# A two-layer diffusion trunk on one core: the order on each engine set by the kernel's own list scheduler

## The chip, the cores and the metric

The kernel runs on one core of a Trainium2 chip. A core has a matrix engine (TensorE, here PE), a vector engine (VectorE, DVE), a scalar engine with function tables (ScalarE, ACT), a general engine (GpSimd, POOL) and a queue that issues most transfers (SyncE, SP). Each engine works through its own list of instructions in the order of the list and waits on semaphores for the others. The metric is the device time of one launch in microseconds; times are medians of several runs. The profile is of one execution of its own.

## The reference: what is computed

Two layers over 512 latent tokens and 256 context tokens of width 1024. Each layer is a mixing part and an MLP, both with RMS norms and modulation vectors made from a conditioning vector. The mixing part projects to four branches (windowed attention A, neighbourhood attention B, and two bidirectional gated recurrences C and D), multiplies each with its branch weights and a gate, adds them, and multiplies with w_out. In the last layer the context is only read.

```
h  = rms_norm(x, ng[0]) * (1 + sc1) + sh1          # hc likewise, for the context
z  = split_in(h @ w_in)                            # queries, keys, values, decays, gates
y  = merge([window(A), neighbourhood(B), recurrence(C), recurrence(D)], z['merge'])
     # merge: sum over j of sigmoid(gate_j) * (branch_j @ w_branch[j]), then @ w_out
x  = x + g1 * rms_norm(y, ng[1])
h2 = rms_norm(x, ng[2]) * (1 + sc2) + sh2
x  = x + g2 * rms_norm(relu(h2 @ w1)**2 @ w2, ng[3])
```

The recurrence of C (4 heads, key width 128) and D (4 heads, key width 64) is a sum over earlier tokens weighted with products of per-channel decays, in both directions.

## The kernel before, in words

Everything is computed by one `Builder`, whose methods issue instructions to `nc.tensor`, `nc.vector`, `nc.scalar`, `nc.gpsimd` and `nc.sync`.

*Weights.* The large weights come as 342 pieces of 128 x 1024 (`wr`), loaded by SP. Each is split into a high part `wh` (ACT, L78, a copy to a rounded format) and a low part `wl` (DVE, L79, the difference). A product is then three passes of matmuls (`mm3`, L433; tiles `pd`): low input by high weight (`hTl,wh`), high by low (`hTh,wl`), high by high (`hTh,wh`). The tiles `hTh` and `hTl` are the normalised tokens, transposed. The MLP's second product goes over `gff` (L1396, tile `y`).

*Norms.* Tokens are normalised in rows (`xn`, DVE L397), transposed on PE (`xT`, L401), scaled by the modulation and split into `hTh` and `hTl` (L414).

*Recurrences.* `d_decays` makes the decays of the d heads on ACT and DVE (tiles `Fe`, `F`, L698 to L705). ACT uses functions of several tables there (exponential, logarithm), and a change of table is an instruction of its own, ACT_TABLE_LOAD. `scan` works on one c head or on two d heads (rows 0 to 63 and 64 to 127 of one tile). It treats tokens in levels of growing distance. At a level, ACT copies the keys `KC` (L563), PE makes for each head one product per block of 128 tokens into the tile `lev` (L579; the two first levels L573 with `pr` and `ones`), DVE rescales `QP` and `KR` by the decays (L583, L584), and DVE copies each head's products by mask into `AT` (L596). There are six blocks in layer 0 and four in layer 1. A matmul on data of four-byte precision with a 128-column output is two PE instructions in the profile.

*Attention B* works on pairs of heads: scores `bS` (PE, L1058 and L1059), the bias table added (DVE, L1063), the maximum `bnm` (DVE, L1065), exponentials `bP` with their sums (ACT, L1068), 1/sum `brl` and scaling (DVE, L1071, L1073), transposes `pT` (PE, L831), the split of the transposed weights into `PTh` (ACT, L834) and `PTl` (DVE, L835), and the output `bO` (PE, L1098).

*Branches.* `pd` from `ysp` and the branch weights is multiplied with its gate into `gates` (DVE, L1165) and added to `acc` (L1166). At the same time DVE makes the modulation vectors of the next part: dot products `mj` of `wm` rows with the conditioning row `cb` (`mod_dot`, L226).

*Order.* Work of one kind is written as Python generators (`self.side`), and the main loop advances them by hand between matmuls (`step`), so that PE has projections to do while a scan or an attention goes on. Tiles come from pools with a fixed number of buffers (PSUM: three `pd`, two `S` tiles of two banks, one `q`). The framework under the kernel takes the program so written, adds the semaphores, and places the instructions of each engine.

## Time and profile before

| | us |
|---|---|
| median of the timed runs (3 runs, 3159.12 to 3166.61) | 3165.26 |
| the profiled execution's own time | 3156.36 |
| its span in the profile | 3154.6 |
| PE busy / DVE busy / ACT busy | 3028.0 / 2074.1 / 1230.0 |
| mean granted clock of PE | 0.994 of full speed |

Busy time is the time in which an engine has at least one instruction in work. "Idle before" in a row is how long the engine stood still ahead of the instruction, and what released it. PEld is PE's loading of weights, which runs beside its products.

### The profile page before, as it was taken

To read this page: it belongs to the slowest core of one execution; us is meant where nothing else is said; L and a number is where in the kernel's file an instruction comes from. 1 tells how busy PE (TensorE), PEld (TensorE's weight loads), DVE (VectorE), ACT (ScalarE), POOL (GpSimd) and SP (SyncE) were. 2 spreads that over 40 slices of the span, in tenths; PEclk is the share of its full clock that TensorE was granted. 3 is DMA by queue.
4 is the path that set the end of the run, shared out by engine and by line. 5 is a ranking of instruction groups with operands and counts; after the bars stand their busy time and mean duration, and the time that the engine had idled before them with its cause. 6 is when DMAs were issued, how large, how long until landed. Compare 5 with 4: busy or idle time off the path is not lost.

```text
span 3154.6 us, 42754 instructions
## 1 busy us (share of the span) xinstructions
PE 3028.0 (96%) x17236; PEld 2746.2 (87%) x17236; DVE 2074.1 (66%) x3313; ACT 1230.0 (39%) x2214; POOL 78.2 (2%) x120
## 2 busy tenths in 40 slices
PE   4999999999989999999999989999999999989998
PEld 3999999999989997898989878898888888778887
DVE  7756675377687666587664555677478577656555
ACT  4523332255525542522222354233256355342222
POOL 1000000000000000000000000000000000000000
PEclk9999999999999999999999999999999999999999
DMA  6111111201252223344331221111221223444332
GB/s 219 61 34 36 46 48 54 71 28 40 81 174 64 74 84 117 118 141 160 121 108 66 88 96 53 42 47 61 83 75 61 91 65 95 155 143 138 98 100 94
DMA packets 77782, 278.21 MB, mean 88 GB/s; under 512 B 9496, under 2 KB 9640, under 8 KB 77584
## 3 DMA queue, kind: packets, MB, share of 16 engines
q1 hardware_dynamic: 74112, 267.47, 25.5%
q0 software_dynamic: 3328, 8.00, 1.3%
q8 instruction: 136, 2.23, 0.3%
q14 instruction: 62, 0.51, 0.1%
q10 hardware_dynamic: 144, 0.01, 0.0%
HBM read 257.08 MB, written 10.49 MB: 85 GB/s over the span
## 4 chain that ended last, share of the span: by engine, by line
PE 46%; DVE 8%; ACT 2%; DMA 2%; issue 2%; POOL 0%; POOLq 0%; DVEq 0%; ACTq 0%; SPq 0%
PE pd L433 27%; PE y L1396 11%; DVE wl L79 1%; PE lev L579 1%; PE o L635 1%; PE pd L1293 1%; DMA wm<-in_wmT 1%; DVE xt L1325 1%; PE pd L1396 1%; DVE mj L226 1%; PE U L616 1%; POOL rstd L387 0%; PE pT L925 0%; PE aO L956 0%; DVE macc L285 0%
## 5 line engine op out<-in xcount | busy, mean ns | idle before, releaser
L433 PE MATMUL pd<-hTh,wl 128*128 128x384 f32 (+2 forms) x2992 | 653.7, 351 | 0.5 <-DVE wl L79 0.5
L433 PE MATMUL pd<-hTl,wh 128*128 128x384 f32 (+3 forms) x2992 | 632.1, 351 | 14.7 <-DVE hTl L414 10.4
L433 PE MATMUL pd<-hTh,wh 128*128 128x384 f32 (+2 forms) x2992 | 615.0, 346 | 0.0
L79 DVE TENSOR_TENSOR wl<-wr,wh 128x1024 fp32r<-128x1024 f32 x342 | 415.0, 1221 | 246.2 <-ACT wh L78 239.0
L433 PEld LDWEIGHTS pd<-hTl,wh 128*128 128x128 f32 (+1 forms) x2992 | 521.7, 189 | 46.5 <-DVE hTl L414 12.5
L433 PEld LDWEIGHTS pd<-hTh,wh 128*128 128x128 f32 x2992 | 529.4, 189 | 26.2 <-issue 0.4
L433 PEld LDWEIGHTS pd<-hTh,wl 128*128 128x128 f32 x2992 | 523.9, 190 | 29.2 <-issue 3.1
L78 ACT ACTIVATE wh<-wr 128x1024 fp32r<-128x1024 f32 x342 | 358.0, 1055 | 413.0 <-PE y L1396 312.7
L1396 PE MATMUL y<-wh,gff 128*128 128x512 f32 x1120 | 300.0, 390 | 0.0
L1396 PEld LDWEIGHTS y<-wh,gff 128*128 128x128 f32 x1120 | 210.2, 188 | 44.5
L1402 DVE TENSOR_TENSOR y<-y,y 128x1024 f32<-128x1024 f32 x130 | 158.1, 1220 | 124.9 <-PE y L1396 124.9
L433 PE MATMUL pd<-ysp,wh 128*128 128x384 f32 (+1 forms) x768 | 179.6, 362 | 17.4 <-DVE gates L1165 14.7
L1396 PE MATMUL y<-wl,gff 128*128 128x512 f32 x560 | 174.2, 391 | 1.9 <-DVE y L1402 1.2
L433 PEld LDWEIGHTS pd<-ysp,wh 128*128 128x128 f32 x768 | 137.5, 190 | 31.5 <-DVE gates L1165 15.9
L1353 ACT ACTIVATE relu<-pd 128x384 f32<-128x384 f32 (+2 forms) x100 | 51.3, 513 | 261.8 <-PE pd L433 261.8
L226 DVE SCALAR_TENSOR_TENSOR mj<-wm,cb 128x1024 f32<-128x1024 f32 x112 | 137.0, 1223 | 9.9 <-DMA wm<-in_wmT 9.0
L1396 PEld LDWEIGHTS y<-wl,gff 128*128 128x128 f32 x560 | 104.5, 188 | 24.9 <-DVE y L1402 3.2
L579 PEld LDWEIGHTS lev<-QP,KC 64*128 64x128 f32 (+1 forms) x960 | 107.6, 189 | 12.5 <-issue 6.7
L579 PE MATMUL lev<-QP,KC 64*128 64x128 f32 (+1 forms) x960 | 115.3, 281 | 3.2 <-DVE QP L584 2.4
L1355 DVE TENSOR_TENSOR relu<-relu 128x384 f32<-128x384 f32 (+2 forms) x100 | 58.1, 582 | 78.7 <-ACT gff L1354 78.7
L596 DVE COPY_PREDICATED AT<-lmask,lev 128x768 f32<-128x768 uint8 (+1 forms) x112 | 97.5, 877 | 10.2 <-PE lev L579 8.3
L387 POOL TENSOR_TENSOR rstd<-rstd,mhalf 128x1 f32<-128x1 f32 (+2 forms) x58 | 47.8, 825 | 1791.3 <-DVE rstd L386 1788.6
(283 smaller groups left out, 4032.0 us busy)
## 6 DMA issues: line engine op xcount, KB each, us to landing
wr<-in_wp SPq DMA_DIRECT2D x342, 512.0 KB, 3.5
wm<-in_wmT SPq DMA_DIRECT2D x64, 512.0 KB, 4.0
wm<-in_wmg SPq DMA_DIRECT2D x32, 512.0 KB, 3.6
xd<-xt SPq DMA_DIRECT2D x16, 512.0 KB, 3.0
xt<-xd SPq DMA_DIRECT2D x14, 512.0 KB, 4.0
btab<-in_btab SPq DMA_DIRECT2D x8, 768.0 KB, 6.9
xt<-in_x SPq DMA_DIRECT2D x8, 512.0 KB, 4.4
bkh<-bkh POOLq DMA_DIRECT2D x16, 192.0 KB, 4.1
```

The lines of the kernel that those rows point to most:

```text
L78: nc.scalar.activation(hi, raw, AF.Copy)
L79: nc.vector.tensor_tensor(lo, raw, hi.bitcast(F32), op=ALU.subtract)
L226: nc.vector.scalar_tensor_tensor(junk, t, 1.0, c, op0=ALU.mult, op1=ALU.mult, accum_out=dst[:, w:w + 1])
L387: nc.gpsimd.tensor_tensor(r[:, :n], r[:, :n], self.mhalf[:, :n], op=ALU.pow)
L433: nc.tensor.matmul(ps[:M, :n], w(k)[:, :M], h(k, t0, n), start=(i == 0), stop=(i == tot - 1))
L579: nc.tensor.matmul(ps[:, c], KC[r0:r0 + dk, c], self.comb_ap(QP[r0:r0 + dk], b, blk, 1), start=True, stop=True)
L596: nc.vector.copy_predicated(at[:, :n].rearrange("p (k t) -> p k t", k=nout), self.lmask[:, lev, None, :].to_broadcast([128, nout, 128]), p ...
L616: nc.tensor.matmul(us[r0:r0 + dk, j * 128:(j + 1) * 128], KT[:, j * 128 + r0:j * 128 + r0 + dk], zs[:, sq[j] * 128:(sq[j] + 1) * 128], sta ...
L1353: nc.scalar.activation(r[:, :m], ps[:, :m], AF.Relu)
L1355: nc.vector.tensor_tensor(r[:, :m], r[:, :m], r[:, :m], op=ALU.mult)
L1396: nc.tensor.matmul(ps, gts[lo + e][:, a_ * NTOK + t * 128:a_ * NTOK + (t + 1) * 128], ws[e][w_][:, h * 512:(h + 1) * 512], start=(i == 0), ...
L1402: nc.vector.tensor_tensor(d, d, ps2, op=ALU.add)
```

## The change

Builder's `nc` becomes a `Recorder`. Every call on one of its five engines is stored as a node instead of being issued. For each node it works out which earlier nodes must come first from the regions of the tiles that are read and written; a PSUM tile counts as one region, and two nodes on different engines that touch the same PSUM tile are ordered even when both read it. It also gives each node an occupancy and a latency from formulas with fixed numbers. When the program is complete, `order()` plays the five engines against these numbers: at each step it takes the engine that can start first, and on it the ready node that stands first in the program. There are two exceptions. On PE, after a matmul that uses at most 64 rows or columns of the array, ready nodes of the same shape go first, those of the half that is free earliest ahead. On ACT, nodes that need no other function table go first, for up to 3 us. `emit()` then issues the nodes in the order found and ties each one to the one ahead of it on its engine, without a semaphore. The formulas decide only the order; they do not change an instruction. In the changed kernel every instruction is issued at one line, L430.

```diff
+SEM = {("PE", "PE"): 0, ("ACT", "PE"): 52, ("DVE", "PE"): 55, ("POOL", "PE"): 54, ("DMA", "PE"): 60}
...
+class Engine:
+    def __getattr__(self, op):
+        rec, f, name = self.rec, getattr(self.real, op), self.name
+
+        def call(*a, **k):
+            rec.add(name, op, f, a, k)
+        return call
...
+    def depend(self, nd, r, w, preds):
+        name, p0, p1, m = r
+        bank = m < 0
...
+            if (w or ow or bank and o.eng != nd.eng) and o is not nd and q0 < p1 and p0 < q1 and (om & m):
...
+            if op == "matmul" and min(rows, m) <= 64 and rhs.dtype == F32:
+
+                nd.shape = "rows" if rows <= 64 else "columns"
+                t = lhs if rows <= 64 else o
+                nd.place = int(t.offset // list(t.ap)[0][0] >= 64)
...
+            nd.table = {"Exp": ("E",), "Tanh": ("E", "S"), "Sigmoid": ("S",), "Ln": ("L",)}.get(str(a[2]).split(".")[-1])
...
+    def order(self):
...
+                if R:
+                    c = (t, R[0][0], R[0][1], e, 0)
+                    if e == "PE" and shape:
+
+                        ok = [(free[N[x[1]].place],) + x for x in R if N[x[1]].shape == shape]
+                        if ok:
+                            c = (t,) + min(ok)[1:] + (e, 0)
+                    if e == "ACT" and N[c[2]].table and table not in N[c[2]].table and t - N[c[2]].ready < 3000:
+
+                        ok = [x for x in R if not N[x[1]].table or table in N[x[1]].table]
+                        if ok:
+                            c = (t,) + min(ok) + (e, 0)
+                elif L:
+                    c = (L[0][0], L[0][1], L[0][2], e, 1)
...
+    def emit(self, tc):
+
+        keep = mybir.DependencyInfo(mybir.DependencyClass.NoSync, mybir.DependencyReason.DATA)
+        last = {}
+        for nd in self.out:
+            f, a, k = nd.emit
+            ins = f(*a, **k).ins
+            if nd.eng in last:
+                tc.add_manual_dep(ins, last[nd.eng], keep, reason="order")
+            last[nd.eng] = ins.name
...
-        self.tc, self.nc, self.a = tc, tc.nc, a
+        self.tc, self.nc, self.a = tc, Recorder(tc.nc), a
...
+            self.nc.order()
+            self.nc.emit(tc)
```

Three places of the order, before and after. The rows give the place in the engine's list, the line, the operation, output<-inputs, the size, and the semaphores waited for.

**PE, the d heads' levels in layer 0**, before. `lev_1083` and `lev_1090` are the products of the two heads at one level; `pd` is a projection of other work.

```order
269 L433 MATMUL pd_1068<-hTh_159,wl_808 128x384 x4
270 L579 MATMUL lev_1083<-QP_950,KC_1081 128x128 [waits DVE_49,Activation_49]
271 L579 MATMUL lev_1083<-QP_950,KC_1081 128x128 x5
272 L579 MATMUL lev_1090<-QP_950,KC_1081 128x128 [waits DVE_49,PE_49]
273 L579 MATMUL lev_1090<-QP_950,KC_1081 128x128 x5
274 L433 MATMUL pd_1068<-hTh_159,wl_808 128x384 x4
275 L433 MATMUL pd_1068<-hTh_159,wh_807 128x384 x8
```

After; here `lev_274` and `lev_275` are the two heads of the same level.

```order
278 L430 MATMUL pd_272<-hTh_125,wl_239 128x384 x4
279 L430 MATMUL lev_274<-QP_256,KC_273 128x128 [waits DVE_49,Activation_49]
280 L430 MATMUL lev_274<-QP_256,KC_273 128x128 x3
281 L430 MATMUL lev_275<-QP_256,KC_273 128x128 [waits DVE_49,PE_49]
282 L430 MATMUL lev_274<-QP_256,KC_273 128x128
283 L430 MATMUL lev_275<-QP_256,KC_273 128x128
284 L430 MATMUL lev_274<-QP_256,KC_273 128x128
285 L430 MATMUL lev_275<-QP_256,KC_273 128x128 x4
286 L430 MATMUL pd_272<-hTh_125,wl_239 128x384 x4
287 L430 MATMUL pd_272<-hTh_125,wh_238 128x384 x8
```

Before, one head's six products stand ahead of the other's. After, the last two of the first head take turns with the first two of the second, and at the level that follows (`lev_277`, `lev_278`) the heads take turns from the first product to the last. The `pd` rows are where they were.

**DVE, attention B in layer 1**, before. `bS_21269` is the unit whose scores get their table here, `pT_21287` the transposes of the unit ahead of it.

```order
2607 L1063 TENSOR_TENSOR bS_21269<-bS_21269,btab_21188 128x2x256 [waits PE_49]
2608 L79 TENSOR_TENSOR wl_21301<-wr_21134,wh_21300 128x1024 [waits DMAHW6_49,Activation_49]
2609 L1065 TENSOR_REDUCE bnm_21222<-bS_21269 128x2 [waits DVE_49]
2610 L1071 RECIPROCAL brl_21283<-bl_21223 128x2 [waits Activation_49]
2611 L1073 TENSOR_SCALAR bP_21270<-bP_21270,brl_21283 128x512 [waits DVE_49]
2612 L1073 TENSOR_SCALAR bP_21270<-bP_21270,brl_21283 128x512
2613 L835 TENSOR_TENSOR PTl_21297<-pT_21287,PTh_21296 128x1024 [waits Activation_49]
2614 L1063 TENSOR_TENSOR bS_21319<-bS_21319,btab_21188 128x2x256 [waits PE_49]
2615 L782 TENSOR_TENSOR bkl_21167<-pd_21306,bkh_21166 64x6x64 [waits Activation_49]
2616 L1065 TENSOR_REDUCE bnm_21222<-bS_21319 128x2 [waits DVE_49]
```

After; the same unit is `bS_3098`, and the transposes ahead of it are `pT_3101`.

```order
2611 L430 TENSOR_TENSOR bS_3098<-bS_3098,btab_3087 128x2x256 [waits PE_49]
2612 L430 TENSOR_REDUCE bnm_3092<-bS_3098 128x2 [waits DVE_49]
2613 L430 TENSOR_TENSOR wl_3105<-wr_3077,wh_3104 128x1024 [waits DMAHW6_49,Activation_49]
2614 L430 TENSOR_TENSOR PTl_3103<-pT_3101,PTh_3102 128x1024 [waits Activation_49]
2615 L430 RECIPROCAL brl_3100<-bl_3093 128x2 [waits Activation_49]
2616 L430 TENSOR_SCALAR bP_3099<-bP_3099,brl_3100 128x512 [waits DVE_49]
2617 L430 TENSOR_SCALAR bP_3099<-bP_3099,brl_3100 128x512
2618 L430 TENSOR_TENSOR bS_3108<-bS_3108,btab_3087 128x2x256 [waits PE_49]
2619 L430 TENSOR_REDUCE bnm_3092<-bS_3108 128x2 [waits DVE_49]
2620 L430 TENSOR_TENSOR bkl_3081<-pd_3107,bkh_3080 64x6x64 [waits Activation_49]
2621 L430 TENSOR_TENSOR PTl_3113<-pT_3111,PTh_3112 128x1024 [waits Activation_49]
```

The maximum `bnm` has moved ahead of the weight split `wl`, and `PTl` of the unit ahead stands in front of `brl` and the scaling of `bP`, not behind them; one `bkl` has moved behind the next unit's scaling.

**DVE, the fourth branch in layer 0**, before. `gates` is the product of a branch's result with its gate, `mj` a dot product for the modulation.

```order
1000 L1166 TENSOR_TENSOR acc_3671<-acc_3671,gates_6825 128x384 [waits DVE_49]
1001 L226 SCALAR_TENSOR_TENSOR mj_7689,mods_96<-wm_7872,cb_7686 128x1024 [waits DVE_49]
1002 L79 TENSOR_TENSOR wl_7915<-wr_7753,wh_7914 128x1024 [waits DMAHW4_49,Activation_49]
1003 L226 SCALAR_TENSOR_TENSOR mj_7689,mods_96<-wm_7891,cb_7685 128x1024 [waits DMAHW4_49,DVE_49]
1004 L1165 SCALAR_TENSOR_TENSOR gates_6826<-gates_6826,pd_7920 128x384 [waits PE_49]
1005 L226 SCALAR_TENSOR_TENSOR mj_7689,mods_96<-wm_7891,cb_7686 128x1024 [waits DVE_49]
1006 L1166 TENSOR_TENSOR acc_3672<-acc_3672,gates_6826 128x384 [waits DVE_49]
```

After; `gates_1044` is the same gate.

```order
997 L430 TENSOR_TENSOR acc_603<-acc_603,gates_1043 128x384
998 L430 SCALAR_TENSOR_TENSOR mj_1182,mods_96<-wm_1207,cb_1180 128x1024 [waits DMAHW3_49,DVE_49]
999 L430 TENSOR_TENSOR wl_1213<-wr_1192,wh_1212 128x1024 [waits DMAHW4_49,Activation_49]
1000 L430 SCALAR_TENSOR_TENSOR mj_1182,mods_96<-wm_1207,cb_1181 128x1024 [waits DVE_49]
1001 L430 SCALAR_TENSOR_TENSOR gates_1044<-gates_1044,pd_1215 128x384 [waits PE_49]
1002 L430 SCALAR_TENSOR_TENSOR mj_1182,mods_96<-wm_1209,cb_1180 128x1024 [waits DMAHW4_49,DVE_49]
1003 L430 TENSOR_TENSOR acc_604<-acc_604,gates_1044 128x384 [waits DVE_49]
```

One `mj` that stood ahead of the `gates` product now stands behind it, and one `acc` addition ahead has moved up.

## Rows read from the trace of the kernel before

**Rows 1.** The page, part 1: busy time, share of the span and instructions per engine.

```profile
PE 3028.0 (96%) x17236; PEld 2746.2 (87%) x17236; DVE 2074.1 (66%) x3313; ACT 1230.0 (39%) x2214; POOL 78.2 (2%) x120
```

**Rows 2.** Windows: stretch, length, busy time per engine (instructions), granted clock, DMA share, GB/s.

```profile
86.00:3100.00 3014.00, 2938.91 (x16823) 2673.70 (x16823) 1976.13 (x3111) 1172.33 (x2104) 65.68 (x94) 0.99 0.26 85
870.00:935.00 65.00, 56.23 (x307) 53.89 (x307) 61.35 (x108) 10.75 (x14) 0.00 (x0) 0.97 0.54 171
935.00:1085.00 150.00, 139.90 (x975) 134.90 (x975) 111.57 (x180) 86.61 (x178) 8.24 (x16) 0.99 0.26 76
1790.00:1915.00 125.00, 110.61 (x569) 97.44 (x567) 74.85 (x128) 71.03 (x118) 7.81 (x12) 0.95 0.29 97
2495.00:2650.00 155.00, 146.70 (x962) 135.78 (x961) 107.48 (x150) 82.11 (x141) 8.16 (x16) 1.00 0.34 87
2735.00:2805.00 70.00, 61.70 (x318) 52.47 (x317) 42.14 (x76) 32.69 (x62) 5.37 (x9) 0.94 0.43 148
```

**Rows 3.** Waits of PE: waiting line, releaser: us in total, times, longest us.

```profile
PE pd L433 <- DVE gates L1165: 15.6, 11, 3.0
PE xT L401 <- DVE xn L397: 11.8, 11, 3.0
...
PE pT L831 <- DVE PTl L835: 7.4, 7, 1.3
PE bS L1058 <- ACT bP L1068: 4.8, 8, 1.2
```

**Rows 4.** Timeline of PE, d then c heads: start us, length us, line, tiles, count.

```profile
121.75 0.98 PE L573 MATMUL lev<-pr,ones 64*128 64x512 f32 x8
...
133.18 2.60 PE L579 MATMUL lev<-QP,KC 64*128 64x128 f32 x24
...
138.02 2.60 PE L579 MATMUL lev<-QP,KC 64*128 64x128 f32 x24
...
371.00 1.50 PE L579 MATMUL lev<-QP,KC 128*128 128x128 f32 x12
...
411.11 0.86 PE L573 MATMUL lev<-pr,ones 128*128 128x512 f32 x4
```

**Rows 5.** Instructions of tile lev: duration ns min/median/max, first and last start us, forms.

```profile
L579 PE MATMUL lev<-QP,KC x960: 270/275/387, 128.2 to 2225.4; 64*128 64x128 f32 x96, 128*128 128x128 f32 x96
```

**Rows 6.** Timeline of DVE between two such runs.

```profile
135.82 0.96 DVE L584 TENSOR_TENSOR QP<-QP,PT 128x768 f32<-128x768 f32 x1
...
136.70 1.02 DVE L596 COPY_PREDICATED AT<-lmask,lev 128x768 f32<-128x768 uint8 x1
```

**Rows 7.** Timeline of attention B, two units, layer 1 [idle before, releaser].

```profile
2542.70 0.69 ACT L1068 ACTIVATE bP<-bS,bnm 128x512 f32<-128x512 f32 x1 [2.49 <-DVE bnm L1065]
...
2543.04 1.20 PE L433 MATMUL pd<-hTh,wh 128*128 128x384 f32 x6
...
2545.19 1.22 DVE L835 TENSOR_TENSOR PTl<-pT,PTh 128x1024 fp32r<-128x1024 f32 x1
...
2550.43 0.39 PE L1058 MATMUL bS<-bkl,bq 128*128 128x256 f32 x1 [0.43 <-ACT bP L1068]
...
2551.53 1.23 DVE L835 TENSOR_TENSOR PTl<-pT,PTh 128x1024 fp32r<-128x1024 f32 x1
...
2552.81 1.09 PE L831 MATMUL pT<-ident,bP 128*128 128x128 f32 x8 [1.16 <-DVE PTl L835]
```

**Rows 8.** Timeline of the branch stage of layer 0.

```profile
912.32 1.23 DVE L226 SCALAR_TENSOR_TENSOR mj<-wm,cb 128x1024 f32<-128x1024 f32 x1
...
914.09 0.96 PE L433 MATMUL pd<-ysp,wh 128*128 128x384 f32 x4 [2.50 <-DVE gates L1165]
...
917.41 0.76 PE L433 MATMUL pd<-hTl,wh 128*128 128x384 f32 x3 [0.94 <-DVE gates L1165]
```

**Rows 9.** Timeline at the decays of the d heads, layer 1.

```profile
1907.48 1.28 ACT L492 ACT_TABLE_LOAD   x1
1907.52 1.00 PEld L433 LDWEIGHTS pd<-hTl,wh 128*128 128x128 f32 x8 [1.71 <-ACT wh L78]
```

320 lines of the change are left out of this document (added).

## The prediction

> **What bounds the kernel now.** I read the page first, then the windows by stage, then the table of waits, and last the timelines of the stages where TensorE (PE) stands idle. The page says that PE is busy 96% of the span, VectorE (DVE) 66% and ScalarE (ACT) 39% [rows 1]. A reordering adds and removes no arithmetic, so it can gain only in two ways: PE's idle time goes, or PE work that now stands one after another runs at once. The span less PE's busy time, 3154.6 - 3028.0, is 126.6 us of idle. Between 86 and 3100 us it is 75 us (the window's length less its PE time); the other 52 us stand at the start, where inputs and modulation vectors are still made, and at the tail. Nine stretches hold 69 of the 75 us: 8.8 us (from 870 us), 10.1 (935), 7.0 (1165), 6.0 (1212), 14.4 (1790), 2.6 (2470), 8.3 (2495), 3.8 (2697) and 8.3 (2735); the rows of five of them stand in [rows 2]. Outside them PE has hardly a hole to fill. In the stretches at 870, 1165 and 2697 us DVE is busy nearly as long as the stretch lasts: there the order of DVE's queue matters, and a better order can only move a wait, since DVE has no spare time. In the others DVE has a quarter to two fifths left and the waits are matters of order alone. The table of waits names them: PE waits 15.6 us for the gate products, 11.8 for the normalised rows xn, 7.4 for PTl and 4.8 for bP [rows 3].
>
> **The change, part by part.** The multiset of instructions on each engine is the same but for five more loads of ACT's function tables. Most matmuls keep their place: the framework's own order was already close to program order, and so is the new one, so a term is earned only where rows really move. The sum is made against the profiled execution (3156.36 us); the median of the timed runs (3165.26) lies 8.9 us above it, and I put the result on the median by taking the same difference off it.
>
> *1. Two heads at once in the level products (lev).* In the d heads these matmuls use 64 rows of the array. One run of two heads with six blocks each is 24 PE instructions in 2.60 us, while a c head, which uses all 128 rows, has 12 in 1.50 us [rows 4]. With one instruction's length (0.275 us, the median [rows 5]) off, the c head starts one every (1.50 - 0.275)/11 = 0.112 us; 24 at that pace would take 23 x 0.112 + 0.275 = 2.85 us. So the run in which all of head 0 stands ahead of all of head 1 saves about two starts, at the one place where the heads meet. The new order lets the heads take turns. That row halves really run side by side is seen in the products one line above: eight 64-row matmuls of two heads take 0.98 us where four 128-row ones take 0.86 [rows 4], an overlap of (2 x 0.86 - 0.98)/0.86 = 86%. Counting pairs of neighbours of different heads in the 24 runs (12 of six blocks, 12 of four) gives 24 before and 126 now. Each such meeting saves a start: 102 x 0.112 = 11.4 us at full overlap. PE has no hole in these stretches, so its time there is the time of the program. What may eat it: after each run DVE has to rescale QP and KR and copy two heads by mask, 0.96 for QP, about as much for KR, 2 x 1.02 for the copies, 3.96 us [rows 6], in a cycle that now lasts 4.84 us (from 133.18 to 138.02). Where heads alternate from the first block, PE would need only about 3.6 to 3.8 us of the cycle, and DVE is then the longer of the two; in the rows where head 0 still goes four blocks ahead, PE needs more and DVE fits. I take **-9 us**; ends 0 and -11.4.
>
> [...]
>
> *2. Attention B.* A unit is scores bS, +table, max (bnm), exponentials (bP), 1/sum, transpose pT, and its split into PTh (ACT) and PTl (DVE). Forty units run in the stretches at 935 and 2495 us, 18.4 us idle in all. In the timeline DVE does a weight split (wl) ahead of bnm, so the exponentials start at 2542.70; PTh comes behind them on ACT, and PTl at 2545.19, behind the 1/sum. In the next unit the score matmuls wait 0.43 us for bP, and the transposes 1.16 us for PTl, which starts only at 2551.53 [rows 7]. In the new order DVE does bnm ahead of wl and PTl ahead of 1/sum, ACT does PTh ahead of the exponentials, and PE puts seven pd matmuls between the scores and the transposes (six take 1.20 us [rows 7]). Following the new rows with the old durations: bnm runs one split (about 1.2 us) earlier and so do the exponentials, PTl ends at about 2543.8 and not at 2546.4, and the transposes find both ready. PTl now stands ahead of 1/sum on DVE, so 1/sum and the scaling wait up to 1.2 us more in the worst case; the seven pd matmuls cover that. I count both named waits as gone, 7.4 + 4.8 = 12.2 [rows 3]: **-12 us**; ends -18.4 (all idle) and +20 (the third rival).
>
> *3. Branch products with the modulation work on DVE* (870, 1165, 2697 us; 19.6 us idle). PE's last pair of waits at 914.09 and 917.41, 2.50 and 0.94 us, ends with gate products that stand behind a 1.23 us modulation dot (mj) [rows 8]. The new order puts one mj fewer ahead of these, about 1.2 us each; in the second stretch the binding ones don't move, in the third by at most 0.4. DVE is full, so what is passed over comes due later. **-2.5 us**; ends +1.2 and -5.
>
> *4. Boundaries between layers* (1212, 1790, 2735 us; 28.7 us idle). The transposes of xn are waited for 11.8 us in eleven places [rows 3], 1.07 on average. Four groups of them now stand behind some eight more matmuls, longer than the mean wait by the pace of six in 1.20 us: 4 x 1.07, so **-4 us**; ends 0 and -15 (half of the idle).
>
> *5. PE's clock.* [...] A sixth, about the share of these waits that goes in 3 and 4, is **-2 us**; ends 0 and -7.
>
> *6. Start and table loads.* At the start DVE does the small operations that wait for the bias table later and starts the modulation dots earlier, and SyncE's writes of the conditioning rows pass the next weight loads, all within 2 us either way: **-1 us**, ends -3 and +2. Five table loads at 1.28 us are 6.4 us of ACT. Most ACT work waits for PE, but at the decays of the d heads ACT's queue holds weight splits that PE waits for, as at 1907.52, 1.71 us, just where a table load stands in its queue [rows 9]. ACT is idle most of the time around it; I take **+0.5 us**, ends 0 and +6.4.
>
> Sum: -9 - 12 - 2.5 - 4 - 2 - 1 + 0.5 = -30 us, 3126 us for an execution like the profiled one, 3135 us for the median.
>
> **Rivals.**
> *Evacuation and full queues bind: about 3160 us.* The lev cycles become DVE's (0 of term 1), stages 3 stay, and attention B gives its waits back in part: about -5 us. For it: DVE needs 3.96 of each 4.84 us cycle, and more with a weight split in it. It also stands for the case that the change does almost nothing, since most rows keep their place. Against it: PE fills the lev cycles with pd matmuls of other work.
> *More goes than I followed: about 3100 us.* Full overlap (11.4), all idle of attention B (18.4), half of the stages 3 and 4 (24), the clock's 7 and 3 at the start, 64 us. For it: in six of the nine stretches no engine is full. Against: DVE is, in three, and I found gains at few waits there.
> *Slower: about 3185 us.* PTl now stands ahead of 1/sum on DVE in the units that I followed; say that it does in all forty. DVE takes its queue in turn. If PTh comes late (ACT has a 1.05 us weight split ahead of it), DVE stands still, 1/sum and scaling wait, and with them the next transposes. At most that is one PTl per unit, 40 x 1.2 = 48 us. The other terms give back 18 (1, 3, 4 and 5). From 0.45 us per unit on, the kernel is no faster; from 0.7 on it is slower by more than a measurement's doubt; I price it at 0.95 us, 38 - 18 = +20. Against it: ACT is idle for 2.49 us ahead of the exponentials in the timeline [rows 7], so that PTh has room.
>
> **How the numbers follow.** Forecast, 3112 to 3155 us: 0.62. More goes: 0.13. Within 0.3% (about 9.5 us, what a measurement of this kernel can tell from no change): 0.14. Slower: 0.11. So faster is 0.62 + 0.13 = 0.75. The range takes in the forecast and most of the first two rivals, 3104 to 3166; above it stand the slower rival and a little of the first, below it half of the second.
>
> **What would show it.** Term 1: the d heads' lev runs of six blocks last 1.4 to 2.2 us instead of 2.60, and their sum falls by about 9; the evacuation rival shows as PE waits on QP in those runs. Term 2: the waits for PTl and bP are near zero; the slower rival shows as PE waiting for the scaled bP in the transposes of both B stretches. Term 3: the wait for gates falls from 15.6 to about 13. Term 4: that for xn from 11.8 to about 7.5. Term 6: PE waits behind splits near 100 and 1900 us if the loads matter. The forecast is wrong if PE's idle time stays above about 120 us, or falls below 80.

## The result, and the profile after

| | before | after |
|---|---|---|
| median of the timed runs, us | 3162.72 (4 runs) | 3092.05 (4 runs, 3091.47 to 3096.00) |
| ratio, 95% interval | | 0.9782 [0.9770, 0.9795] |
| the profiled execution / its span, us | 3156.36 / 3154.6 | 3091.47 / 3089.5 |

The kernel became 2.2% faster. The forecast was 3135 us, with a range from 3104 to 3166: the direction is right, and the time lies below the range. What came is close in total to the second rival, "more goes than I followed", at 3100 us, though not part by part. The forecast was put on a median of three runs of the kernel before, 3165.26; a fourth run took that median to 3162.72.

The page's line of busy times, of the changed kernel (share of the span, instructions), answers to [rows 1]:

```profile
PE 2999.0 (97%) x17236; PEld 2733.8 (88%) x17236; DVE 2069.3 (67%) x3313; ACT 1233.6 (40%) x2219; POOL 77.4 (3%) x120
```

The profiled executions differ by 64.9 us, their spans by 65.1. PE's busy time fell by 29.0 (from 3028.0), its idle time by 36.1 (from 126.6 to 90.5). So more than half is idle time that went, and the rest is PE work that takes less time: 11.0 us of it the level products, part of the rest the clock.

Windows of the changed kernel: stretch, length, then busy time of PE, PEld, DVE, ACT and POOL (instructions), granted clock, DMA share, GB/s. Each is cut at the same count of PE matmuls as the stretch of before that starts at 870, 935, 1790, 1850, 2495 and 2735 us [rows 2]:

```profile
856.40:919.60 63.20, 56.14 (x308) 54.13 (x307) 60.88 (x104) 10.96 (x14) 0.00 (x0) 0.97 0.55 175
919.60:1057.20 137.60, 136.92 (x974) 133.10 (x973) 111.77 (x185) 87.98 (x179) 8.16 (x16) 1.00 0.30 84
1756.70:1812.20 55.50, 50.62 (x260) 42.62 (x259) 47.18 (x93) 30.59 (x64) 7.54 (x11) 1.00 0.44 152
1812.20:1871.40 59.20, 54.26 (x311) 49.29 (x310) 28.50 (x38) 42.40 (x60) 0.55 (x1) 1.00 0.19 63
2443.00:2588.00 145.00, 144.65 (x961) 136.18 (x960) 107.25 (x149) 83.24 (x141) 8.17 (x16) 1.00 0.35 94
2672.00:2740.00 68.00, 61.72 (x317) 52.49 (x316) 43.06 (x77) 32.91 (x62) 4.43 (x8) 0.94 0.46 155
```

In the two stretches of attention B (from 919.60 and 2443.00 us) PE is now busy to within 0.7 us of the whole length. The first took 150 us before and takes 137.60, the second 155 and 145.00. In the two stretches at the boundary between the layers the granted clock is 1.00, where the whole stretch from 1790 us showed 0.95 [rows 2]. The branch stretch (856.40) is little shorter, and the boundary in layer 1 (2672.00) by 2 us only.

Waits of PE after (line, releaser: us in total, times, longest us) answer to [rows 3]:

```profile
PE pd L430 <- DVE hTl L430: 16.3, 13, 4.8
PE pd L430 <- DVE gates L430: 13.6, 9, 3.2
...
PE bS L430 <- ACT bP L430: 0.2, 1, 0.2
...
PE pT L430 <- DVE PTl L430: 0.2, 1, 0.2
```

The waits for PTl and bP are gone (7.4 and 4.8 before). That for xn, 11.8 before, has no row any more. What remains are mainly the gates and the low part of the normalised tokens, `hTl`, which had 18.0 before in these two rows of its waits:

```profile
PE pd L433 <- DVE hTl L414: 10.4, 5, 3.3
...
PE pd L475 <- DVE hTl L375: 7.6, 9, 3.5
```

The level products of the d heads in the changed kernel, PE's timeline (start us, length us), answer to [rows 4]:

```profile
122.16 1.71 PE L430 MATMUL lev<-QP,KC 64*128 64x128 f32 x24
...
126.11 2.31 PE L430 MATMUL lev<-QP,KC 64*128 64x128 f32 x24
...
130.63 1.63 PE L430 MATMUL lev<-QP,KC 64*128 64x128 f32 x24
...
134.47 2.34 PE L430 MATMUL lev<-QP,KC 64*128 64x128 f32 x24
...
139.38 2.16 PE L430 MATMUL lev<-QP,KC 64*128 64x128 f32 x24
```

The runs last 1.63 to 2.34 us where they lasted 2.60. From the start of one to the next it takes 3.95, 4.52, 3.84 and 4.91 us, on average 4.31, where one such cycle of before took 4.84.

One unit of attention B after, all engines (idle before and releaser in brackets), answers to [rows 7]:

```profile
2487.89 1.03 ACT L430 ACTIVATE PTh<-pT 128x1024 fp32r<-128x1024 f32 x1 [0.24 <-PE pT L430]
2488.89 1.21 DVE L430 TENSOR_TENSOR wl<-wr,wh 128x1024 fp32r<-128x1024 f32 x1
...
2489.01 0.69 ACT L430 ACTIVATE bP<-bS,bnm 128x512 f32<-128x512 f32 x1
...
2490.02 1.22 DVE L430 TENSOR_TENSOR PTl<-pT,PTh 128x1024 fp32r<-128x1024 f32 x1
...
2490.67 0.28 PE L430 MATMUL bS<-bkl,bq 128*128 128x256 f32 x1
...
2491.63 1.41 PE L430 MATMUL pd<-hTh,wh 128*128 128x384 f32 x7
...
2492.87 1.03 PE L430 MATMUL pT<-ident,bP 128*128 128x128 f32 x8
```

ACT makes PTh ahead of the exponentials, DVE starts PTl at 2490.02 in the gap behind a weight split, and it ends at 2491.24. The transposes at 2492.87 find everything ready, and so do the scores at 2490.67. The seven pd matmuls stand between.

The whole difference, stage by stage (both traces cut at the same PE matmuls; us, and of it PE's idle time), by the terms of the prediction:

| term | forecast | profiled executions |
|---|---|---|
| 1 level products | -9 | -11.0 (PE time of `lev`) |
| 2 attention B, two stretches | -12 | -22.1 (idle -17.4, PE time -4.8) |
| 3 branches (870, 1165, 2697) | -2.5 | -2.6 (-2.0, +0.7, -1.3) |
| 4 and 5 boundaries (1212, 1790 to 1930, 2735) and clock | -6 | -18.1 (-3.6, -4.5, -6.0, -2.1, -1.9; idle -9.5) |
| 6 start, up to 86 us | -1 | -6.0 |
| rest, net | 0 | -5.1 (of it +2.7 at 560 to 870) |

### The profile page after: what moved, and what is told of

Its sections match the earlier page's. It is cut to its first block, busy times and chain, and to the rows that moved or that the text cites. A ratio compares the mean times of both kernels' runs of the same rounds, so it can differ in the third digit from the quotient of the medians.

```text
span 3089.5 us, 42764 instructions
## 1 busy us (share of the span) xinstructions
PE 2999.0 (97%) x17236; PEld 2733.8 (88%) x17236; DVE 2069.3 (67%) x3313; ACT 1233.6 (40%) x2219; POOL 77.4 (3%) x120
## 4 chain that ended last, share of the span: by engine, by line
PE 86%; DVE 9%; ACT 3%; issue 1%; DMA 0%; POOL 0%; SPq 0%; DVEq 0%; POOLq 0%; ACTq 0%
PE pd L430 59%; PE y L430 12%; PE lev L430 4%; PE o L430 2%; PE pT L430 2%; DVE mj L430 1%; DVE wl L430 1%; PE bO L430 1%; PE aS L430 1%; PE U L430 1%; PE bS L430 1%; DVE asm L430 1%; PE aO L430 1%; DVE acc L430 1%; DVE macc L430 1%
## 5 line engine op out<-in xcount | busy, mean ns | idle before, releaser
L430 PE MATMUL pd<-hTl,wh 128*128 128x384 f32 (+3 forms) x3032 | 647.2, 351 | 24.5 <-DVE hTl L430 16.3
L430 PE MATMUL pd<-hTh,wl 128*128 128x384 f32 (+3 forms) x3032 | 664.6, 349 | 0.0
L430 PE MATMUL pd<-hTh,wh 128*128 128x384 f32 (+3 forms) x3032 | 629.2, 346 | 0.0
L430 DVE TENSOR_TENSOR wl<-wr,wh 128x1024 fp32r<-128x1024 f32 x342 | 414.8, 1220 | 286.0 <-ACT wh L430 277.6
L430 PEld LDWEIGHTS pd<-hTl,wh 128*128 128x128 f32 (+1 forms) x3032 | 528.1, 189 | 59.8 <-DVE hTl L430 21.1
L430 PEld LDWEIGHTS pd<-hTh,wh 128*128 128x128 f32 (+1 forms) x3032 | 535.6, 188 | 25.9
L430 PEld LDWEIGHTS pd<-hTh,wl 128*128 128x128 f32 (+1 forms) x3032 | 529.5, 189 | 27.6 <-issue 2.7
L430 ACT ACTIVATE wh<-wr 128x1024 fp32r<-128x1024 f32 x342 | 358.0, 1056 | 421.5 <-PE y L430 317.2
L430 PE MATMUL y<-wh,gff 128*128 128x512 f32 x1120 | 299.8, 389 | 0.0
L430 PEld LDWEIGHTS y<-wh,gff 128*128 128x128 f32 x1120 | 210.3, 188 | 44.1
L430 DVE TENSOR_TENSOR y<-y,y 128x1024 f32<-128x1024 f32 x130 | 158.0, 1219 | 121.3 <-PE y L430 121.3
L430 PE MATMUL pd<-ysp,wh 128*128 128x384 f32 (+1 forms) x768 | 180.1, 363 | 15.6 <-DVE gates L430 12.9
L430 PE MATMUL y<-wl,gff 128*128 128x512 f32 x560 | 173.5, 390 | 0.0
L430 PEld LDWEIGHTS pd<-ysp,wh 128*128 128x128 f32 x768 | 138.4, 192 | 28.9 <-DVE gates L430 13.0
L430 ACT ACTIVATE relu<-pd 128x384 f32<-128x384 f32 (+2 forms) x100 | 51.3, 513 | 259.2 <-PE pd L430 259.1
L430 DVE SCALAR_TENSOR_TENSOR mj<-wm,cb 128x1024 f32<-128x1024 f32 x112 | 136.5, 1218 | 10.9 <-DMA wm<-in_wmT 10.2
L430 PEld LDWEIGHTS y<-wl,gff 128*128 128x128 f32 x560 | 104.9, 188 | 21.1 <-ACT xn L430 0.6
L430 PE MATMUL lev<-QP,KC 64*128 64x128 f32 (+1 forms) x960 | 104.2, 280 | 0.0
L430 PEld LDWEIGHTS lev<-QP,KC 64*128 64x128 f32 (+1 forms) x960 | 98.3, 189 | 6.4 <-issue 5.4
L430 DVE TENSOR_TENSOR PTl<-pT,PTh 128x512 fp32r<-128x512 f32 (+2 forms) x120 | 95.3, 794 | 12.3 <-ACT PTh L430 10.6
L430 DVE COPY_PREDICATED AT<-lmask,lev 128x768 f32<-128x768 uint8 (+1 forms) x112 | 96.7, 878 | 5.1 <-PE lev L430 4.9
L430 ACT ACTIVATE PTh<-pT 128x512 fp32r<-128x512 f32 (+2 forms) x120 | 81.9, 682 | 43.2 <-PE pT L430 42.3
```

The source lines that it names most:

```text
L430: ins = f(*a, **k).ins
```

## The experiments

All times are medians; each ratio is to the kernel before, run beside it on the same chip.

Most experiments are **hybrids**. The changed kernel keeps, as a table, the order that each engine had before; stretches of an engine's list take the order that `order()` finds. With no stretch it has the order of before on all engines, with all of them that of after. A stretch counts instructions of the engine's list (the table and the body of `mix()` are left out here):

```diff
+SPANS = {"PE": [[5040, 6013], [13140, 14100]], "DVE": [[1070, 1248], [2672, 2821]], "ACT": [[624, 765], [1593, 1709]], "POOL": [[30, 46], [86, 102]], "SP": [[135, 147], [387, 406]]}
...
+            for a, b in SPANS[e]:
+                old[a:b] = mine[a:b]
...
             self.nc.order()
+            self.nc.mix()
             self.nc.emit(tc)
```

**One part of the order alone.** The stretches above are the two of attention B.

> The order of before on every engine, but in the two stretches of attention B (935 to 1085 and 2495 to 2650 us of before) that of the changed kernel on all five engines. Theory 1 (the gain of a stretch is made by the order in that stretch, and keeps): 22 us less than before, PE idle in the two stretches from 18.4 to about 1 us, and 4 to 5 us less of busy time, since a matmul that follows a wait starts slower. Rival, my own term: only the two waits that I named go, 12 us less. Rival 2 (later stages take it back): under 8 us less.

Measured: 3136.95 against 3160.92 us, 0.9923 [0.9907, 0.9938]. The two stretches shortened by 12.1 and 9.8 us, idle by 9.2 and 7.9, as in the full change. The new order of attention B is worth 22 to 24 us by itself.

The boundaries between norms and projections:

```diff
+SPANS = {"PE": [[6743, 7189], [9613, 10216], [14518, 14837]], "DVE": [[1368, 1474], [1800, 1936], [2901, 2976]], "ACT": [[835, 903], [1087, 1187], [1760, 1810]], "POOL": [[48, 60], [62, 74], [103, 112]], "SP": [[171, 197], [298, 321], [428, 448]]}
```

> The order of before, but at the layer boundaries (1212 to 1310, 1790 to 1923, 2735 to 2805 us of before) that of the changed kernel. Theory 1: 16 us less than before; about 9 of idle time, and about 7 because PE's clock no longer falls to its lower level between 1848 and 1922 us. Rival (the clock holds in the changed kernel for another reason than the order at the boundary): about 9 us less, and the clock falls there as before.

Measured: 3145.60 against 3160.92 us, 0.9949 [0.9935, 0.9964]. The stretches from 1212, 1790, 1850, 1915 and 2735 us shortened by 3.4, 4.5, 4.6, 1.5 and 1.7. PE's waits in this hybrid:

```profile
PE pd L497 <- DVE hTl L497: 19.9, 14, 4.8
...
PE xT L497 <- DVE xn L497: 0.3, 1, 0.3
```

The wait for xn is gone, all but 0.3 us of 11.8, and the wait for hTl, 18.0 before, took back only 1.9. The clock's falls of before at 1838 and 1855 us (to a granted clock of 0.50, for 3.4 and 6.8 us) went too; the one at 1909 us (0.50 for 3.4 us) stayed. The window of before over the last two shows what they cost:

```profile
1850.00:1915.00 65.00, 58.10 (x311) 53.52 (x310) 27.95 (x38) 41.93 (x59) 0.55 (x1) 0.92 0.17 57
```

PE's busy time there is 58.10 us at 0.92, and 54.26 at 1.00 for as many matmuls after (second boundary window above): 3.8 of the 6.0 us of this stretch are busy time that went with the clock's falls.

The scans (115 to 560 and 1923 to 2240 us):

```diff
+SPANS = {"PE": [[387, 2791], [10216, 11799]], "DVE": [[140, 513], [1936, 2300]], "ACT": [[95, 300], [1187, 1359]], "POOL": [[18, 26], [74, 81]], "SP": [[45, 81], [321, 353]]}
```

> The order of before, but from 115 to 560 and from 1923 to 2240 us of before, the stretches with the scans of the c and d heads, that of the changed kernel. Theory 1: 16 to 17 us less than before, 11 of it in the lev products of the d heads whose two heads take turns, the rest idle time ahead of c heads and small gains in pd. Rival (evacuation binds when the rest of the order is that of before): under 8 us, with new PE waits on QP or AT.

Measured: 3147.35 against 3160.92 us, 0.9958 [0.9942, 0.9973], 13.6 us. By stage -3.5, -4.4, -2.4, -2.7 and -2.4: the level products' 11 and a few microseconds of other waits.

The start, to 86 us:

```diff
+SPANS = {"PE": [[0, 220]], "DVE": [[0, 124]], "ACT": [[0, 71]], "POOL": [[0, 18]], "SP": [[0, 41]]}
```

> The order of before, but up to 86 us of before that of the changed kernel. Theory 1: 6 us less than before: the first matmul 2 us earlier, and 4 us less before the first projections. Rival (the start is bound by the input transfers, and what is early there waits later): 0 to 2 us less.

Measured: 3157.09 against 3160.92 us, 0.9989 [0.9979, 0.9999]; in its trace the first matmul comes at 17.9 us and not at 19.8, and the stage up to 46 us is another 3.8 shorter.

The four hybrids gain 24.0, 15.3, 13.6 and 3.8 us, together 56.7 of the 70.7 between the medians. By their traces the same stages gained 61.7 of 64.9 us in the full change. The parts nearly add up; the remainder was not cut finer, except for the branches:

```diff
+SPANS = {"PE": [[4734, 5040], [6547, 6743], [13031, 13140], [14380, 14518]], "DVE": [[993, 1070], [1310, 1368], [2650, 2672], [2858, 2901]], "ACT": [[610, 624], [824, 835], [1577, 1593], [1739, 1760]], "POOL": [[30, 30], [48, 48], [86, 86], [103, 103]], "SP": [[112, 135], [160, 171], [382, 387], [413, 428]]}
```

> The order of before, but in the four branch stretches (870 to 935, 1165 to 1212, 2470 to 2495, 2697 to 2735 us of before) that of the changed kernel; PE's order does not differ there. Theory 1: 2.5 us less than before, as in the table by stretches, so not told apart from it by the timing but by the idle time in the four stretches (22.1 us, now about 18.5). Rival (DVE is full, what is passed over comes due in the next stretch): the gain comes back as idle time at 935 or 1212.

Measured: 3161.53 against 3161.42 us, 1.0002 [0.9992, 1.0012]. The stages moved by -2.1, -1.1, 0 and +2.4 us, and two later ones by +1.5 and +1.7. PE's idle time in the four stages fell from 22.1 to 19.7 us (18.5 was expected), and 1.3 of it came back in the stage from 935 us, as the rival has it. The whole time can't tell the two apart; its interval leaves the branches' new order anything between 2.5 us gained and 3.8 lost.

**Attention B: whose order?** The same two stretches, with only PE's order of after, or only the other engines':

```diff
+SPANS = {"PE": [[5040, 6013], [13140, 14100]], "DVE": [], "ACT": [], "POOL": [], "SP": []}
```

> The order of before, but in the two stretches of attention B PE alone follows the changed kernel; DVE and ACT keep the order of before. Theory (the waits come from where DVE and ACT put bnm, PTh and PTl; PE's moves only cover): no gain or a loss, -2 to +15 us against before, since PE comes to scores and output products earlier than bP and PTl are ready. Rival (PE's own order, pd behind the scores, is what removes the waits): 12 us or more less than before.

Measured: 3160.35 against 3160.93 us, 1.0000 [0.9990, 1.0009]; the stages moved by +0.3 and +5.6 us in its trace, so no gain at best. This run and that of the branches issue almost the whole order of before through the Recorder, and agree with the kernel before to 0.1% (1.0000 and 1.0002). So the way of issuing by itself is worth nothing beyond some 3 us; the gain is the order's.

```diff
+SPANS = {"PE": [], "DVE": [[1070, 1248], [2672, 2821]], "ACT": [[624, 765], [1593, 1709]], "POOL": [[30, 46], [86, 102]], "SP": [[135, 147], [387, 406]]}
```

> The order of before, but in the two stretches of attention B DVE, ACT and the transfer queues follow the changed kernel; PE keeps the order of before. Theory: most of the gain, 12 to 20 of the 22 us; what is left is PE waiting at the places where the moved pd matmuls would have stood. Rival (PE's order removes the waits): under 6 us less than before.

Measured: 3145.72 against 3160.93 us, 0.9952 [0.9937, 0.9967]; the stages -7.7 and -6.7. Waits of PE with PE's order alone (us in total, times, longest us):

```profile
PE pT L497 <- DVE PTl L497: 10.4, 10, 1.9
...
PE bS L497 <- ACT bP L497: 5.3, 10, 0.8
```

The same view with the other engines' order alone:

```profile
PE bO L497 <- DVE yb L497: 4.7, 5, 1.5
...
PE pT L497 <- DVE PTl L497: 0.5, 2, 0.3
...
PE bS L497 <- ACT bP L497: 0.4, 1, 0.4
```

The order on DVE and ACT removes the two named waits; PE's alone makes them longer. With PE in its old order another wait, of the outputs bO for yb (earlier outputs that DVE adds up), holds 4.7 us, where it was 2.5 before. So the gain of 24 is 15 from DVE and ACT, and 9 more when PE's order moves with them, though it brings nothing alone.

**The planner's rules.** First the rule by which PE stays with one shape:

```diff
-                    if e == "PE" and shape:
+                    if False and e == "PE" and shape:
```

> The changed kernel without its rule that matmuls of 64 rows or columns go in turns of the free half: the neighbours of different heads in the lev runs are 24 again and not 126, and little else moves. Theory (the lev gain is two heads at once, full overlap): 11 us more than the changed kernel, about 3103 if that is 3092, with the lev runs of six blocks at 2.60 us. Rival (evacuation or other work would have hidden part of it): 3 to 6 us more.

Measured: 3102.31 us, 0.9817 [0.9802, 0.9832], 10.3 above after. The level products stand head after head again, and a run has its old length:

```profile
127.42 2.60 PE L430 MATMUL lev<-QP,KC 64*128 64x128 f32 x24
```

The meetings of two heads fell from 126 to 24, and PE's time on `lev` is 133.7 us, against 123.5 after and 134.5 before. So the rule's worth is term 1.

Second, the rule by which ACT puts off a change of function table:

```diff
-                    if e == "ACT" and N[c[2]].table and table not in N[c[2]].table and t - N[c[2]].ready < 3000:
+                    if False and e == "ACT" and N[c[2]].table and table not in N[c[2]].table and t - N[c[2]].ready < 3000:
```

> The changed kernel without its rule that ACT prefers work of the loaded function table. The order still has 16 table loads, so both theories expect nothing for the loads; 116 and not 126 meetings of the two heads in lev would cost about 1 us. Within 2 us of the changed kernel. Rival: the rule keeps ACT's work together elsewhere and its loss costs 5 us or more.

Measured: 3094.39 us, 0.9791 [0.9776, 0.9806]; not told apart from after. The number of table loads (16) stayed the same: the rule decides almost nothing here, and no run shows what the five more loads cost.

Third, the rule by which two engines that only read one PSUM tile are still put one behind the other:

```diff
-            if (w or ow or bank and o.eng != nd.eng) and o is not nd and q0 < p1 and p0 < q1 and (om & m):
+            if (w or ow) and o is not nd and q0 < p1 and p0 < q1 and (om & m):
```

> The changed kernel whose planner no longer counts a PSUM tile as one thing that one engine uses at a time (two engines that only read it are not ordered in the plan; the waits that the program needs are set as before). The order changes at some 1100 places of PE and 530 of DVE. Theory (the gain comes from planning with durations, the PSUM rule is a detail): within 6 us of the changed kernel. Rival (the rule is what keeps DVE and ACT from standing in each other's way in attention B, where PTh and PTl read the same tile): 10 us or more above it, with waits for PTl and bP back.

Measured: 3133.57 against 3160.18 us, 0.9921 [0.9900, 0.9942], 41 us above after: the most expensive single rule to lose. Without the rule the planner plans as if both engines could go at once. In the trace they still take turns: where a norm's eight transposed blocks are scaled, four on DVE and four on ACT, no block of the one engine overlaps one of the other in any of the sixteen norms (start us, length us, idle before and releaser):

```profile
1848.33 0.41 DVE L430 TENSOR_SCALAR xn<-xT,mods 128x128 f32<-128x128 f32 x1 [0.53 <-ACT xn L430]
1848.78 0.46 ACT L430 ACTIVATE xn<-xT,mods 128x128 f32<-128x128 f32 x1 [0.48 <-DVE xn L430]
1849.27 0.41 DVE L430 TENSOR_SCALAR xn<-xT,mods 128x128 f32<-128x128 f32 x1 [0.53 <-ACT xn L430]
1849.71 0.46 ACT L430 ACTIVATE xn<-xT,mods 128x128 f32<-128x128 f32 x1 [0.48 <-DVE xn L430]
```

Each stands idle while the other works. DVE's waits for ACT's block are 26.8 us in 47 places here and 5.0 in 13 after. The round of eight blocks itself is shorter here, 3.6 us on average, than after (5.3) or before (5.7): the planner that knows the rule doesn't shorten the round, it puts other work between the turns. Here all that stands behind a round waits for the whole of it. Just before, PE stood 8.39 us for a copy, `qk`, which had such a round (1835.32 to 1838.91) and six more operations ahead of it in ACT's list:

```profile
1843.68 1.97 PE L430 MATMUL pd<-hTl,wh 128*128 128x384 f32 x5 [8.39 <-ACT qk L430]
```

ACT's wait for DVE's block (xn) is 45.0 us in 52 places (33.0 in 30 after). Against after this kernel lost 17.5 us from 1790 to 1915 us, 10.5 at 1212, 6.1 and 5.7 in the stretches of attention B and 1.5 from 560 us. Its profiled execution shows 59.2 us at the lower clock level (granted clock 0.50), that of after 32.0, and PE's busy time is 12.6 us longer; so some 13 of the 41 us are, by estimate, PE running slower, not waiting.

No run here lets the two engines read the tile at once, so what that would do is not shown.

**Is the turn itself the cost?** The blocks of a norm in two halves, four on DVE and then four on ACT, in the kernel before and in the changed one:

```diff
         for k in range(8):
-            if k % 2:
+            if k >= 4:
```

> The kernel before with one edit, in norm_h: the scaling of the eight transposed blocks goes to DVE for blocks 0 to 3 and to ACT for 4 to 7, not in turns. ACT and DVE read the same PSUM tile there and are never in it at the same time; in turns that is up to eight changes of engine for each tile, each of which waits for whatever stands ahead on the other engine's list, now it is one. Theory (these changes of engine make hTl and xn late at the layer boundaries of the kernel before, and the planner's PSUM rule is what takes them into account): ACT's waits for DVE xn fall from 48 us to under 15, the boundaries lose 5 to 12 us, 5 to 12 us less than before. Rival (the boundary is bound by the norm's own chain, and the changes of engine lie beside it): within 3 us.

Measured: 3149.09 against 3161.42 us, 0.9965 [0.9952, 0.9979]: 12 us by the medians for one changed condition. A norm's round of eight blocks takes 3.0 us on average over the sixteen norms, where it took 5.7. ACT's wait for DVE's blocks in the kernel before:

```profile
ACT xn L405 <- DVE xn L408: 48.3, 41, 5.2
```

And in the same kernel with halves:

```profile
ACT xn L405 <- DVE xn L408: 19.8, 8, 3.9
```

Under 15 was expected. PE's waits for xn and for this hTl, 11.8 and 10.4 us before, are with halves:

```profile
PE xT L401 <- DVE xn L397: 7.7, 10, 2.1
...
PE pd L433 <- DVE hTl L414: 4.0, 2, 3.1
```

The stages at 1212, 1790 and 2735 us shortened by 3.8, 4.7 and 3.0, all three among those that the new order shortens; the stage from 1850 us, 6.0 shorter in the new order, did not move. Of the 3.0 a part is clock: 4.2 us at the lower level (0.50) there, 8.2 before. ACT starts on its half only when DVE has ended its last block, in all sixteen norms, though each has its own 512 columns of the tile; ACT's row above puts 19.8 us of its waits, in 8 places, down to DVE's blocks. What sets this order is not shown, and whether the two halves could run at once was not tried.

The same edit in the changed kernel:

> The changed kernel with the same edit in norm_h. Theory: the planner has already put other work between the changes of engine, so less is left: 0 to 6 us less than the changed kernel, with the wait for hTl (16.3 us) smaller. Rival: same as in the kernel before, 5 to 12 us less.

Measured: 3095.60 us, 0.9794 [0.9778, 0.9809], no gain on after. ACT's waits fell there as well (33.0 to 20.3 us) and PE's for hTl from 16.3 to 10.8, but a wait for xn of 4.4 us came back, and the stages at 1790 and 1850 us grew by 2 and 3.9, with falls of the clock that after doesn't have there (granted clock 1.00 in both; the mean of the profiled execution is 0.993 here, 0.995 after). That the new order had already taken what the halves give fits this; it isn't shown apart from the clock.

**Two trials for a better order.** The one long stretch that got worse, 560 to 870 us, in the old order, everything else in the new:

```diff
+SPANS = {"PE": [[0, 2791], [4734, 16360]], "DVE": [[0, 513], [993, 3191]], "ACT": [[0, 300], [610, 1944]], "POOL": [[0, 26], [30, 116]], "SP": [[0, 81], [112, 523]]}
```

> The changed kernel with the order of before from 560 to 870 us of before (attention A of layer 0), the one stretch in which the changed kernel was slower, by 2.7 us. Theory 1 (the gain or loss of a stretch belongs to its own order): 2 to 3 us less than the changed kernel. Rival (its loss comes from what the stretches ahead hand over): no difference.

Measured: 3090.91 us, 0.9784 [0.9764, 0.9804]. The stretch is 2.7 us shorter than after and its idle fell from 2.96 to 1.20; in the whole time it can't be told from after.

Modulation dots (mj) ranked 150 nodes later, so that gate products go first:

```diff
+            nc.prio = len(nc.nodes) + 150 if nc.nodes and nc.nodes[-1].i > 3000 else 0
             nc.vector.scalar_tensor_tensor(junk, t, 1.0, c, op0=ALU.mult, op1=ALU.mult, accum_out=dst[:, w:w + 1])
+        nc.prio = 0
```

> The changed kernel, but the planner ranks the modulation dots mj after layer 0's first scans 150 places later, so that gate products go ahead of them whenever both are ready; in the branch stages of layer 0 fewer mj stand between gates. Theory (the waits for gates are queueing behind mj, and DVE has room for mj in the stretches that follow): the wait for gates falls from 13.6 to under 7 us and the time by 4 to 8 us. Rival (DVE is full there and its work has to be done: the wait moves to weight splits or accsp, or the buffers of wm come free too late): within 2 us or slower.

Measured: 3085.85 us (3082.49 to 3089.77), 0.9772 [0.9748, 0.9795], the lowest median of all, with an interval that overlaps that of after. The windows from 870 and 935 us of before, in this kernel, show more than the whole time does:

```profile
856.30:909.40 53.10, 53.10 (x309) 53.10 (x308) 50.12 (x85) 10.55 (x13) 0.00 (x0) 1.00 0.49 153
909.40:1049.10 139.70, 138.59 (x975) 132.63 (x974) 122.81 (x204) 88.59 (x179) 8.21 (x16) 1.00 0.38 105
```

And of PE's waits in this kernel, the row of the gates:

```profile
PE pd L430 <- DVE gates L430: 7.2, 5, 3.0
```

The branch stretch lost all of its 7.06 us of idle and the clock's fall with it (granted clock 0.97 to 1.00), 63.20 to 53.10 us; the next one paid back 2.1. Nineteen DVE instructions (104 to 85) went from the one to the other. The wait for gates is 7.2 us, 13.6 after.

The later dots and the norm's halves together:

> The changed kernel with both the later rank of the modulation dots and the edit in norm_h. The two act in different stretches, so both theories expect their sum: 3086 less what the edit alone gives in the changed kernel, 3080 to 3086, faster than both kernels.

Measured: 3088.35 us, 0.9769 [0.9753, 0.9784]; the halves add nothing here either (3080 to 3086 was expected), and the stages at 1790 and 1850 us grew by the same 2.1 and 3.9.

## Why the prediction missed

**What held.** The gain lies in the stretches that [rows 2] names and in the level products. Term 1 is right in mechanism and nearly in size: -9 forecast, -11.0 in the trace, 10.3 by removing the rule. Its upper end was 11.4. The first rival, that DVE's evacuation binds the cycles, fell: nearly all of the full overlap was obtained, and from 115 to 370 us PE is idle nowhere (0.85 us before). Of the four cycles from 122.16 us, whose starts are shown above, these are the first and the last (window, length, then busy time of PE, PEld, DVE, ACT and POOL):

```profile
122.16:126.11 3.95, 3.95 (x38) 3.56 (x37) 2.82 (x4) 1.34 (x2) 0.00 (x0) 1.00 0.02 4
...
134.47:139.38 4.91, 4.91 (x40) 4.53 (x39) 4.91 (x6) 1.10 (x2) 0.00 (x0) 1.00 0.26 82
```

PE is busy throughout both; DVE has 1.1 us left in the first, less work than the 3.96 us that the prediction put into each cycle, and none in the last. The third rival's wait, of the transposes for the scaled bP, didn't come: all of PE's idle time in the two stretches of attention B is 1.0 us.

**Term 2, -12 for -22: a step that failed.** The mechanism held. The mis-sized step is "I count both named waits as gone", 12.2 us. The other 6.1 of the 18.4 us stood in the same table of waits as [rows 3], in four rows that the prediction doesn't count:

```profile
PE bO L1098 <- DVE yb L1109: 2.5, 4, 0.9
...
PE bS L1058 <- DVE bVl L1031: 1.5, 3, 0.7
...
PE bO L1098 <- DVE PTl L835: 1.2, 3, 0.4
...
PE bS L1058 <- DMA bkl<-bkl: 0.9, 1, 0.9
```

These went too, all but 1.0 us, and PE's idle fell by 17.4. PE's busy time fell by a further 4.8 in the same matmuls, which was not in the sum at all: even the end of -18.4 was too near. The two runs with half of the order show that reading one engine's rows could not give this: DVE's and ACT's order gives 15 us, and 9 more come only when PE's order moves as well.

**Terms 4 and 5, -6 for -18 by stage (15.3 by the hybrid): the other step that failed.** I costed the xn wait as "4 x 1.07", the four groups whose place on PE had visibly moved. All of it went, 11.8 to nothing, and the hybrid kept it so. What the prediction lacks is a cause behind the waits of these stages: DVE and ACT taking turns on the transposed tile. ACT waited 48.3 us in 41 places for DVE there, a row that the prediction doesn't use. The statement of the change says plainly that two readers of a PSUM tile are put in order, and the prediction gave this no term. Shorter rounds in the kernel before give 12 us, with 4.1 us less of PE's wait for xn and 6.4 less for hTl; leaving the rule out of the planner loses 41. The turns are not the whole cause: with halves 7.7 us of the wait for xn stay, which only the new order took. Of the clock's share, by the granted clocks of [rows 2] 0.03 x 65 + 0.05 x 125 + 0.06 x 70, about 12 us, the prediction took a sixth everywhere; no run shows such an even share. It went as a whole from 1790 to 1930 us, where PE was busy for 12.0 us at the lower level (granted clock 0.50) before and for none after, about 6 us by half of that, and not at all at 870 and 2735 us, where the granted clock is 0.97 and 0.94 as before. At 1165 us, which the term doesn't have, a longer fall (10.24 us at 0.50, 3.41 before) took some 2 us back, by the same estimate.

**Term 3, -2.5 for -2.6: the size partly by chance, and the reason wrong.** The wait for the gates fell from 15.6 to 13.6 us, as forecast, but the three stages agree with the sum only together: one lost 0.7 us where nothing was to move, one gained 1.3 where 0.4 was the most. "DVE is full, so what is passed over comes due later" does not hold as a bound: in the run that puts the dots later, 10 us went from a stretch where DVE was busy 60.88 of 63.20, and only 2.1 were paid back in the next. DVE was full with work that was not needed there yet. After and this kernel differ in no instruction.

**Term 6, -1 for -6.** The start was judged by the queue order "within 2 us either way". The first matmul came 2.0 us earlier, and the waits behind it shrank: the hybrid of the start is 3.8 us faster by the median, 5.7 by its trace. The sign for the table loads, PE waiting behind splits near 100 and 1900 us, didn't show: the wait at 1907.52 us [rows 9] is gone, and the longest wait for a split, 5.0 us, stands at 34.67 us, where no table is loaded. No run takes the loads away, so their cost stays open.

**The sum and the range.** The forecast was built from rows that could be seen to move: "a term is earned only where rows really move". A planner that moves thousands of rows also removes waits outside those rows; every term came out at its size or above, and none of the losses that the rivals priced appeared. Of the 30 us some 19 were idle time of PE and 11 busy time; 36.1 and 29.0 went. So half of what is missing is busy time, and the prediction's own sign of being wrong, idle time above 120 or below 80 us, did not show: it is 90.5.

Beside the 11.0 us of the level products an estimate can be made of two parts. PE was busy for 31.7 us at a granted clock of 0.50 before and for 21.2 after, about 5 us by half of the difference. And the first `pd` matmul behind a wait took 0.43 us, the sixth 0.34 (means of eleven places in the trace of before); waits of over 0.15 us went from 98 to 56, which makes about 4 us.

"More goes" stood at 3100 us with 0.13, and the range ended at 3104. Its parts did not come as priced either: of the 24 us of idle in stages 3 and 4 about 13 went, and the difference is busy time.

**Open.** These estimates leave some 9 of the 29.0 us of busy time without a cause. In attention B they leave less: 24 waits fewer make 2.4 us there, and the 3.4 us at the lower level that only the kernel before has there make 1.7, together 4.1 of the 4.8. Open are also the 14 us of the medians' difference that the four hybrids together don't hold (6 by the traces of their own stages): with intervals of 3 to 5 us each way, it may be the sum of small gains elsewhere or in part the clock, whose time at the lower level differs from one execution to the next.

## What to carry to other kernels

Look at the waits of engines that are not the bottleneck when they share a PSUM tile: two readers that took turns block by block were coupled here (ACT stood 48.3 us for DVE's blocks), and PE's waits showed what came late, not the turns that made it late. Try a half for each, or an order that puts other work between the turns. A full engine in a stretch isn't a bound until one has asked whether its work is due there. When an order is changed as a whole, add up all waits of a stretch and not the one or two whose rows can be followed, and take the whole idle time as the end and not as the estimate: 17.4 of 18.4 us went in attention B, 9.5 of 28.7 at the boundaries and 3.6 of 19.6 in the branches. And give the matrix engine's busy time a term of its own: here it fell by 29.0 us as its idle time fell by 36.1.
